# Attention weights times values: one F32 product replaced by three F32R products of rounded parts

## The chip, the cores and the metric

The kernel runs on one core of one Trainium2 chip. The metric is the device time of one execution in microseconds (us). The engines of the core are TensorE (PE, matrix products; its weight loads are listed apart as PEld), VectorE (DVE), ScalarE (ACT), GpSimd (POOL) and SyncE (SP, which issues DMAs). SBUF is the memory on the chip that the engines compute from, PSUM the one that PE writes its products to, in banks of 128 partitions x 512 F32 numbers.

## The reference, cut to what matters

One layer of an encoder over two request groups with the same weights, 2048 and 256 tokens, 2304 in all, width 1024. A projection feeds two mixers, an mLSTM with 8 heads and an attention with 8 query heads over 2 key/value heads (64 channels each), whose outputs are concatenated and projected back; then comes a feed-forward part with a convolution of width 3. The change is in the attention:

```python
def block(qi):
    s = jnp.einsum('bqhgd,bkhd->bhgqk', qi, k).astype(jnp.float32) * scale
    p = jax.nn.softmax(s, axis=-1)
    return jnp.einsum('bhgqk,bkhd->bqhgd', p.astype(v.dtype), v)
```

All of it is in float32, and attention goes over all keys of a request group.

## The kernel before, in words

The work has four phases. Phase A (`phase_a`) normalises the input and computes queries, keys, values and gates, one tile of 128 tokens after the other; it writes them to DRAM (`q_d`, `k_d`, `v_d`). Then attention (`attention`) and mLSTM (`mlstm`) run side by side as two Python generators which `run_both` advances by turns by estimated costs, the mLSTM ahead by a factor `LEAD`; once the mLSTM's program is through, steps of phase C (`phase_c`, output projection) take its place, and the attention's steps get a higher priority. Phase D (`phase_d`) is the feed-forward part. The order of instructions on each engine isn't written out: a scheduler makes it at build time from the dependencies, the priorities and a simulated timeline. On the chip each engine then takes its instructions strictly in that order, and waits on semaphores. A tile with `bufs=n` is a ring of n buffers: the next use waits for the last reader of the use n before it.

Nearly all products are made as F32R products of split operands: an operand x becomes hi = x rounded to F32R (an ACT copy into a tile of that type) and lo = x - hi (a DVE subtraction), and hi*hi + hi*lo + lo*hi are added up in PSUM. An F32 product, as the attention used for weights times values, is one call in the program, and the trace shows it as two matmul instructions with a weight load each.

The attention goes through 36 blocks of 512 queries: in each of the two key/value groups 16 large ones (one head, 4 tiles of 128 queries, 16 key tiles) and 2 small ones (two heads, 2 tiles each, 2 key tiles). `load_kv` (L440 on) brings a group's keys and values from DRAM in parts of 4 key tiles, on POOL's queue, in this order for each part: keys twice (L459), the keys' lo part (L460), values (L462). For the first large group it first writes one element of every tile (L456), which ties the loads to the end of the maxima of the first block. `vv` holds 64 channels of values and 64 columns of ones, so that a product yields the weighted sum in partitions 0 to 63 and the sum of the weights in 64 to 127.

For a block, `prep` transposes the queries, and `maxstep` (L512) makes one product of 128 queries by 512 keys (L516) and its row maximum on DVE (L517). These are done for the next block while the current one runs. `prep2` puts the negative maxima into row 64 of `qm`. `scores` (L532) takes a pair of key tiles at a time: two products each into a PSUM tile `ps` (L539, L540), then the exponential on ACT into `pe` in SBUF (L541). `values` (L544) follows `PLAG` = 2 pairs later and adds the pair to `pv` (L551). `px`, `ps`, the transposed queries and the spread maxima share a ring of `SCB` = 4 PSUM banks. At a block's end `fin1` copies sums and weight sums to SBUF (L559, L560), and `fin2`, which is called in the next block, takes the reciprocal of the weight sums on DVE (L564), multiplies on POOL (L565) and stores.

The mLSTM beside it uses one PSUM buffer (`mj`, `MJ` = 1) for its projections, which ACT copies out (L660 to L672), and short chains of small DVE, ACT and POOL steps.

Of the kernel before, what the change touches and what calls it, by code (L numbers as in the profile page):

```python
# [9 lines left out]
F32 = mybir.dt.float32  # L10
F32R = mybir.dt.float32r
AF = mybir.ActivationFunctionType
ALU = mybir.AluOpType
# [4 lines left out]
P = 128  # L18
# [4 lines left out]
NT = T // P  # L23
NT1 = T1 // P
HD = 64
# [43 lines left out]
RW = 4  # L69
PO = 4  # L70
PB = 4
PEB = 5
PLAG = 2
ZT = 3
SG = 3
# [10 lines left out]
def f32(ap):  # L86
    return ap.bitcast(F32)
# [6 lines left out]
def rstd_of(g, pool, ms, n, name):  # L94
    nc = g.nc
    r = pool.tile([P, n], F32, tag="rstd", name=name)
    nc.gpsimd.tensor_scalar(r, ms, EPS, None, ALU.add)
    nc.gpsimd.tensor_tensor(r, r, g.mhalf[:, 0:n], ALU.pow)
    return r
# [38 lines left out]
def phase_a(g, tc, sw, st_x, after_x, after_mm, after_pj):  # L138


    nc = g.nc
    with ExitStack() as st:
        sp = st.enter_context(tc.tile_pool(name="a_s", bufs=2, reuse_waits="tile"))
# [72 lines left out]
        def mm(*tiles):  # L216

            pjs = [pj_.tile([P, 1024], F32, tag="pj", name=f"pj{i}", bufs=2) for i in tiles]
            cols = ((0, 512), (512, 800))
            if tiles[0] == order[0]:  # L220
                steps = [(t, z, c) for c in range(NCC) for t in range(len(tiles)) for z in cols]
            else:
                steps = [(0, z, c) for z in cols for c in range(NCC)]
            for t, (c0, c1), c in steps:
                for k, (a, b) in enumerate(((0, 0), (0, 1), (1, 0))):
                    nc.tensor.matmul(pjs[t][:, c0:c1], nTs[tiles[t]][:, c, a, :], ws[c][:, b, c0:c1],  # L226
                                     start=(c == 0 and k == 0), stop=(c == NCC - 1 and k == 2))
            for i in tiles:
                nTs.pop(i)
            return pjs  # L230

        def post1(i, pj):
            qk = sp.tile([P, 10, HD], F32, tag="qk", name=f"qk{i}")
            nc.scalar.activation(qk, pj[:, 0:640].rearrange("p (h d) -> p h d", d=HD), AF.Copy)
            v = sp.tile([P, 2, HD], F32, tag="v", name=f"v{i}", bufs=2)
            nc.scalar.activation(v, pj[:, 640:768].rearrange("p (h d) -> p h d", d=HD), AF.Copy)
            nc.scalar.dma_start(g.v_d[:, :, i, :].rearrange("g p d -> p g d"), v)
            gt = g.gtm[:, i]
            nc.vector.tensor_tensor(gt, pj[:, 768:800].rearrange("p (a k) -> p a k", a=2),
                                    bgb.rearrange("p (a k) -> p a k", a=2), ALU.add)  # L240
            xh = sp.tile([P, 10, HD], F32, tag="xh", name=f"xh{i}", bufs=1)
            nc.scalar.activation(xh, qk, AF.Square, scale=0.125)
            ms = sp.tile([P, 10], F32, tag="ms10", name=f"ms10_{i}")
            nc.vector.tensor_reduce(ms, xh, AX.X, ALU.add)
            r = rstd_of(g, sp, ms, 10, f"rqk{i}")
            nc.vector.tensor_tensor(xh, qk, r.unsqueeze(2).to_broadcast([P, 10, HD]), ALU.mult)
            ti = i % NT1
            t1 = sp.tile([P, 10, HD], F32, tag="t1", name=f"t1_{i}")
            t2 = sp.tile([P, 10, HD], F32, tag="t2", name=f"t2_{i}", bufs=1)
            for a, (h0, h1) in enumerate(((0, 8), (8, 10))):  # L250
                n = h1 - h0
                nc.vector.tensor_tensor(t1[:, h0:h1, :], xh[:, h0:h1, :],
                                        tab[:, ti, a, 0:1, :].to_broadcast([P, n, HD]), ALU.mult)
                for q in range(2):
                    def half(t, z):
                        return t.rearrange("p h (r z f) -> p h r z f", r=2, z=2)[:, :, :, z, :]
                    sin = tab[:, ti, a, 1:2, :].rearrange("p h (r z f) -> p h r z f", r=2, z=2)[:, :, :, q, :]
                    nc.gpsimd.tensor_tensor(half(t2[:, h0:h1, :], q), half(xh[:, h0:h1, :], 1 - q),
                                            sin.to_broadcast([P, n, 2, 16]), ALU.mult)
            nc.vector.tensor_tensor(t1, t1, t2, ALU.add)  # L260
            qz = sp.tile([P, 8, P], F32R, tag="qz", name=f"qz{i}", bufs=2)
            nc.scalar.activation(qz[:, :, 0:HD], t1[:, 0:8, :], AF.Copy)
            nc.vector.tensor_tensor(qz[:, :, HD:P], t1[:, 0:8, :], f32(qz[:, :, 0:HD]), ALU.subtract)
            g.st.dma_start(g.q_d[:, i].rearrange("h p d -> p h d"), f32(qz))
            kz = sp.tile([P, 2, P], F32R, tag="kz", name=f"kz{i}", bufs=1)
            nc.scalar.activation(kz[:, :, 0:HD], t1[:, 8:10, :], AF.Copy)
            nc.vector.tensor_tensor(kz[:, :, HD:P], t1[:, 8:10, :], f32(kz[:, :, 0:HD]), ALU.subtract)
            return kz
# [41 lines left out]
        for n, i in enumerate(order):  # L310
            pj, = mm(i)
# [115 lines left out]
def attention(g, tc, s1, s2, pp):  # L427


    nc = g.nc  # L430
    sp = s1
# [8 lines left out]
    def load_kv(grp, k0, k1, after=None):  # L440

        if (grp, k0) in kv:
            return
        n = k1 - k0
        sp = s2 if n == NT1 else s1
        kv[(grp, k0)] = parts = []
        for t0 in range(0, n, 4):
            m = min(4, n - t0)
            s = f"{n}_{t0}"
            kk = sp.tile([P, m * P], F32R, tag="kk" + s, name=f"kk{grp}_{s}", bufs=1)  # L450
            kl1 = sp.tile([65, m * P], F32R, tag="kl1" + s, name=f"kl1{grp}_{s}", bufs=1)
            vv = sp.tile([P, m, P], F32, tag="vv" + s, name=f"vv{grp}_{s}", bufs=1)
            c = slice((k0 + t0) * P, (k0 + t0 + m) * P)
            if after is not None:
                for t in (kk[0:1, 0:1], kk[HD:HD + 1, 0:1], kl1[0:1, 0:1], vv[0:1, 0, 0:1]):
                    nc.gpsimd.tensor_copy(t, after[0:1, 0:1])  # L456
            nc.gpsimd.memset(vv[:, :, HD:P], 1.0)
            for r in (0, HD):
                nc.gpsimd.dma_start(f32(kk[r:r + HD, :]), g.k_d[grp, 0:HD, c])  # L459
            nc.gpsimd.dma_start(f32(kl1[0:HD, :]), g.k_d[grp, HD:P, c])  # L460
            nc.gpsimd.memset(f32(kl1[64:65, :]), 1.0)
            nc.gpsimd.dma_start(vv[:, :, 0:HD], g.v_d[grp, :, k0 + t0:k0 + t0 + m])  # L462
            parts.append((kk, kl1, vv))

    class HB:
        pass
# [64 lines left out]

    def scores(s, kp):  # L532
        N = s.N
        pe = sp.tile([P, 2, 512], F32, tag="pe", name=f"pe{s.nm}_{kp}", bufs=PEB)
        for z in range(2):
            ps = pp.tile([P, 512], F32, tag="sc", name=f"ps{s.nm}_{kp}_{z}")
            kk, kl1, _ = s.kv[kp // 2]
            kc = (2 * kp + z) % 4 * P
            nc.tensor.matmul(ps[:, 0:N], kk[:, kc:kc + P], s.qq[:, 0:N], start=True, stop=False)  # L539
            nc.tensor.matmul(ps[:, 0:N], kl1[:, kc:kc + P], s.qm[:, 0:N], start=False, stop=True)  # L540
            nc.scalar.activation(pe[:, z, 0:N], ps[:, 0:N], AF.Exp)  # L541
        return kp, pe

    def values(s, kp, pe):  # L544

        N = s.N
        if kp == 0:
            s.pv = pp.tile([P, 512], F32, tag="pv", name="pv" + s.nm, bufs=1)
        for z in range(2):
            kt = 2 * kp + z  # L550
            nc.tensor.matmul(s.pv[:, 0:N], s.kv[kp // 2][2][:, kt % 4, :], pe[:, z, 0:N], start=(kt == 0),  # L551
                             stop=(kt == s.nk - 1))

    def fin1(s):

# [5 lines left out]

    def fin2(s):
        N = s.N
        nc.vector.reciprocal(s.rs[:, 0:N], s.rs[:, 0:N])  # L564
        nc.gpsimd.tensor_tensor(s.o1[:, 0:N], s.o1[:, 0:N], s.rs[:, 0:N], ALU.mult)  # L565
        for t0, (h, q0, q1) in part(s):
            r0 = HD * (h % 2)
            nc.gpsimd.dma_start(g.mix_d[q0 // 2:q1 // 2, r0:r0 + HD, 4 + h // 2].rearrange("n p t -> p n t"),
                           s.o1[:, t0 * P:(t0 + q1 - q0) * P].rearrange("p (n t) -> p n t", t=BT))
            if h == 7:  # L570
                g.mixed.update(range(q0, q1))
# [8 lines left out]
    for n in range(len(hbs)):  # L580
# [25 lines left out]
        if nxt is not None and nxt.todo:  # L606
            while nxt.todo:
                maxstep(nxt)
            prep2(nxt)
        old, cur = cur, nxt  # L610
    fin2(old)


# [628 lines left out]
def body(tc, aps, phases="abcd"):  # L1242
    nc = tc.nc
    g = Ctx()
# [3 lines left out]
    with ExitStack() as st:  # L1248
        dp = st.enter_context(tc.tile_pool(name="dram", bufs=1, space=DRAM))
        kp = st.enter_context(tc.tile_pool(name="konst", bufs=1))  # L1250
# [4 lines left out]
        def dram(name, shape):  # L1255
            setattr(g, name, dp.tile(shape, F32, name=name))
# [4 lines left out]
        dram("x1_d", [NB, P, NCC, BT])  # L1261
        dram("q_d", [8, NT, P, P])
        dram("k_d", [2, P, T])
        dram("v_d", [2, P, NT, HD])
        dram("nm_d", [NT, 16, P])
        dram("og_d", [4, NB, P, 2, P])
        g.ident = kp.tile([P, P], F32, name="ident")
# [155 lines left out]
```

## Time and profile before

| | |
|---|---|
| Runs | 3506.89, 3509.6, 3512.7 us; median 3509.6 us |
| Profiled execution, span from first to last instruction | 3509.1 us (no other time is given for it) |
| PE busy | 3406.8 us, 97% |
| DVE busy | 2345.9 us, 67% |
| ACT busy | 1683.3 us, 48% |
| POOL busy | 1144.3 us, 33% |
| Products of weights and values (L551) | 1040 instructions, 271.9 to 1812.4 us |

How to read it: times are from one execution. A group of instructions is given as line, engine, operation, what it writes and reads, their shapes and the count; behind the first bar stand the time in which one of the group was busy and the mean duration in ns, behind the second the idle time of the engine just before them and what ended it. The ends of matmuls are modelled and overlap the next one's start, so the pace of products is read from their starts. The strips of digits are the busy share in 40 equal slices of the span, in tenths. A row of stretches has the stretch, its length, the busy time of PE, PEld, DVE, ACT and POOL (with counts of instructions), the granted PE clock as a share of full speed, the DMA engines' share and GB/s.

### The profile page before, as it was taken

Reading aid. Unit: us, or ns where it says so; the run is one execution under the profiler, and the core shown is the slowest. Engines: PE = TensorE matmul, PEld = TensorE weight load, DVE = VectorE, ACT = ScalarE, POOL = GpSimd, SP = SyncE. Lnnn points to the kernel's source line nnn. Section 1 sums busy time; section 2 is a strip of 40 time slices with the busy share of each in tenths; the row PEclk is TensorE's granted clock in tenths of the full one; section 3 lists DMA queues with packets and bytes.
Section 4 is the critical chain, followed back from the end, with each engine's and each line's share of the span. In section 5 each row is a group of like instructions: output and inputs, shape, how many; then the busy total and the mean of one; then the engine's idle time right before and its main releaser. Section 6 shows DMA issues by size and latency. Waiting matters only on the chain.

```text
span 3509.1 us, 53243 instructions
## 1 busy us (share of the span) xinstructions
PE 3406.8 (97%) x19538; PEld 3031.7 (86%) x19538; DVE 2345.9 (67%) x3962; ACT 1683.3 (48%) x3827; POOL 1144.3 (33%) x1362
## 2 busy tenths in 40 slices
PE   7889999999999999999999999999999999999998
PEld 6787787777777777767789999999999999999998
DVE  7773365546544555664444887878888879887777
ACT  5434454444444454453332544445544445655555
POOL 7863022213231322311135333224433224422222
PEclk9999999999999999999999999999999999999999
DMA  7765233233243434442247323213323213312211
GB/s 234 209 188 147 89 107 100 92 108 106 84 123 111 137 114 133 126 147 80 88 147 252 125 97 103 73 67 123 137 98 108 73 67 123 135 64 73 73 67 54
DMA packets 288917, 401.76 MB, mean 114 GB/s; under 512 B 27408, under 2 KB 188976, under 8 KB 288656
## 3 DMA queue, kind: packets, MB, share of 16 engines
q1 hardware_dynamic: 256560, 355.87, 30.9%
q0 software_dynamic: 10640, 31.86, 3.2%
q10 hardware_dynamic: 21456, 10.62, 1.0%
q8 instruction: 154, 2.52, 0.3%
q14 instruction: 107, 0.88, 0.1%
HBM read 315.55 MB, written 82.72 MB: 113 GB/s over the span
## 4 chain that ended last, share of the span: by engine, by line
PE 75%; DVE 9%; issue 5%; POOL 4%; DMA 4%; ACT 3%; SPq 0%; POOLq 0%; DVEq 0%; ACTq 0%
PE pa L1034 12%; PE pv L551 11%; PE pd L1172 11%; PE pc L1034 6%; PE po L918 5%; PE mv L668 4%; PE mj L658 4%; PE ps L539 3%; PE ps L540 3%; PE px L516 3%; PE pb L1034 3%; PE mN L794 1%; PE mj L684 1%; DVE acc L1174 1%; DVE y L1128 1%
## 5 line engine op out<-in xcount | busy, mean ns | idle before, releaser
L1172 PE MATMUL pd<-act,wd 128*128 128x384 f32 (+1 forms) x3120 | 592.0, 336 | 19.2 <-DVE acc L1174 10.8
L1172 PEld LDWEIGHTS pd<-act,wd 128*128 128x128 f32 x3120 | 540.0, 188 | 26.0 <-DVE acc L1174 14.5
L551 PE MATMUL pv<-pe,vv 128*128 128x512 f32 x1040 | 514.4, 593 | 0.2
L517 DVE TENSOR_REDUCE mx<-px 128x1 f32<-128x512 f32 (+1 forms) x528 | 342.8, 673 | 196.6 <-PE px L516 194.9
L1034 PE MATMUL pa<-nt,wut 128*128 128x386 f32 (+2 forms) x2376 | 454.7, 339 | 2.2 <-ACT u L1050 2.2
L1034 PEld LDWEIGHTS pa<-nt,wut 128*128 128x128 f32 x2376 | 422.2, 190 | 2.5 <-ACT u L1050 2.5
L541 ACT ACTIVATE pe<-ps 128x512 f32<-128x512 f32 x520 | 292.7, 595 | 266.2 <-PE ps L540 262.4
L1039 POOL TENSOR_TENSOR tw<-ru 128x512 f32<-128x512 f32 x66 | 102.1, 1547 | 740.3 <-DMA ru<-w_up 598.6
L1128 DVE SCALAR_TENSOR_TENSOR y<-u,cw,y 128x768 f32<-128x768 f32 (+1 forms) x264 | 308.9, 1171 | 35.8 <-ACT y L1121 28.8
L1174 DVE TENSOR_TENSOR acc<-pd,acc 128x384 f32<-128x384 f32 (+1 forms) x544 | 281.5, 538 | 40.1 <-PE pd L1172 38.1
L1050 ACT ACTIVATE u<-pa 128x386 f32<-128x386 f32 (+2 forms) x264 | 128.8, 488 | 328.3 <-PE pa L1034 325.8
L551 PEld LDWEIGHTS pv<-pe,vv 128*128 128x128 f32 x1040 | 189.0, 189 | 82.8 <-issue 58.3
L539 PE MATMUL ps<-qq,kk 128*128 128x512 f32 x520 | 249.5, 483 | 0.9 <-ACT pe L541 0.6
L918 PE MATMUL po<-cmx,wo 128*128 128x256 f32 x1728 | 242.5, 291 | 1.6 <-DVE wo L107 1.6
L918 PEld LDWEIGHTS po<-cmx,wo 128*128 128x128 f32 x1728 | 222.3, 191 | 24.7 <-issue 17.1
L516 PE MATMUL px<-kk,qq 128*128 128x512 f32 (+1 forms) x528 | 224.5, 455 | 2.7 <-ACT pe L541 1.3
L658 PE MATMUL mj<-mn,wm 128*128 128x256 f32 x1296 | 213.2, 305 | 8.6 <-ACT og L672 4.6
L658 PEld LDWEIGHTS mj<-mn,wm 128*128 128x128 f32 x1296 | 181.8, 194 | 38.0 <-issue 21.1
L540 PE MATMUL ps<-qm,kl 65*128 65x512 f32 x520 | 207.4, 402 | 0.1
L668 PE MATMUL mv<-wm,mn 128*128 128x256 f32 x1296 | 205.0, 298 | 0.4 <-ACT qb L664 0.4
L668 PEld LDWEIGHTS mv<-wm,mn 128*128 128x128 f32 x1296 | 178.1, 192 | 21.6 <-issue 13.9
L226 PE MATMUL pj<-w_a,n1T 128*128 128x512 f32 (+1 forms) x864 | 180.2, 363 | 8.6 <-DVE n1T L184 6.0
(285 smaller groups left out, 6663.8 us busy)
## 6 DMA issues: line engine op xcount, KB each, us to landing
ru<-w_up SPq DMA_DIRECT2D x132, 512.0 KB, 3.2
mn<-n_d SPq DMA_DIRECT2D x216, 256.0 KB, 3.3
rd<-w_down SPq DMA_DIRECT2D x66, 512.0 KB, 3.3
n_d<-n1T SPq DMA_DIRECT2D x18, 1024.0 KB, 5.2
dm<-nm_d POOLq DMA_DIRECT2D x72, 256.0 KB, 3.6
mjn<-n_d SPq DMA_DIRECT2D x72, 256.0 KB, 2.9
mvn<-n_d SPq DMA_DIRECT2D x72, 256.0 KB, 3.2
q_d<-qz SPq DMA_DIRECT2D x18, 512.0 KB, 5.6
```

The lines of the kernel that those rows point to most:

```text
L516: nc.tensor.matmul(ps[:, 0:w], s.qq[:, t * P:(t + 1) * P], s.kv[z0][0][:, 0:w], start=True, stop=True)
L517: nc.vector.tensor_reduce(s.mx[:, t, z0:z0 + 1], ps[:, 0:w], AX.X, ALU.max)
L539: nc.tensor.matmul(ps[:, 0:N], kk[:, kc:kc + P], s.qq[:, 0:N], start=True, stop=False)
L540: nc.tensor.matmul(ps[:, 0:N], kl1[:, kc:kc + P], s.qm[:, 0:N], start=False, stop=True)
L551: nc.tensor.matmul(s.pv[:, 0:N], s.kv[kp // 2][2][:, kt % 4, :], pe[:, z, 0:N], start=(kt == 0), stop=(kt == s.nk - 1))
L658: nc.tensor.matmul(pj[:, o], s.w[c][:, a, o * P:(o + 1) * P], nT[c][:, h, :], start=(c + o + k == 0), stop=(c == NCC - 1 and k == 2 and o ...
L668: nc.tensor.matmul(pv[:, o], nT[c][:, a, o * P:(o + 1) * P], s.w[c][:, h, 256:512], start=(c + o + k == 0), stop=(c == NCC - 1 and k == 2 ...
L918: nc.tensor.matmul(po[:, o], wo[c][z // 2][:, a, n], mx[c][:, h, :], start=(c == 0 and k == 0), stop=(c == NCC - 1 and k == 2))
L1034: nc.tensor.matmul(p, w[:, aa, c, :], ops[k][:, c, bb, 0:n], start=c == 0 and i == 0 and not add, stop=c == NCC // 2 - 1 and i == 2, skip_ ...
L1128: nc.vector.scalar_tensor_tensor(y[:, s:e], u[:, s + k:e + k], cw[:, k, jj:jj + 1], y[:, s:e], ALU.mult, ALU.add)
L1172: nc.tensor.matmul(po, wds[j][c // 4][:, aa, c % 4 * P:(c % 4 + 1) * P], acts[j][:, bb, z0:z1], start=(j == 0 and k == 0), stop=(j == len( ...
L1174: nc.vector.tensor_tensor(accs[c][:, z0:z1], po, accs[c][:, z0:z1], ALU.add)
```

## The change

- *Weights.* `pe` is now a ring of 3 single key tiles (it was 5 pairs, thus 10 tiles). Behind each exponential ACT copies `pe` to `x[:, 0]`, rounded to F32R, and DVE writes pe - `x[:, 0]` to `x[:, 1]`. `x` is a ring of `XB` = 6 tiles under the tag `px`.
- *Values.* Phase A rounds a tile's values on ACT and subtracts on DVE from PSUM; `v_d` holds both parts. `load_kv` loads the rounded part into `vv` and the remainder into `vl` (64 columns, no ones), with one more DMA and, where L456 applies, one more copy for each part.
- *Products.* For each key tile three F32R products are added to `pv`: `vv` by hi, `vl` by hi (into partitions 0 to 63 alone), `vv` by lo. The product of the two remainders is left out.
- *Reciprocals.* `fin2` takes the reciprocal in four pieces of 128 columns.

```diff
-PEB = 5
+PEB = 3
+XB = 6
...
-            v = sp.tile([P, 2, HD], F32, tag="v", name=f"v{i}", bufs=2)
-            nc.scalar.activation(v, pj[:, 640:768].rearrange("p (h d) -> p h d", d=HD), AF.Copy)
-            nc.scalar.dma_start(g.v_d[:, :, i, :].rearrange("g p d -> p g d"), v)
+            v = sp.tile([P, 2, 2, HD], F32R, tag="v", name=f"v{i}", bufs=2)
+            pv = pj[:, 640:768].rearrange("p (h d) -> p h d", d=HD)
+            nc.scalar.activation(v[:, :, 0], pv, AF.Copy)
+            nc.vector.tensor_tensor(v[:, :, 1], pv, f32(v[:, :, 0]), ALU.subtract)
+            nc.scalar.dma_start(g.v_d[:, :, i].rearrange("g p a d -> p g a d"), f32(v))
...
-            vv = sp.tile([P, m, P], F32, tag="vv" + s, name=f"vv{grp}_{s}", bufs=1)
+            vv = sp.tile([P, m, P], F32R, tag="vv" + s, name=f"vv{grp}_{s}", bufs=1)
+            vl = sp.tile([P, m, HD], F32R, tag="vl" + s, name=f"vl{grp}_{s}", bufs=1)
...
-            nc.gpsimd.dma_start(vv[:, :, 0:HD], g.v_d[grp, :, k0 + t0:k0 + t0 + m])
-            parts.append((kk, kl1, vv))
+            for a, t in ((0, vv[:, :, 0:HD]), (1, vl)):
+                nc.gpsimd.dma_start(f32(t), g.v_d[grp, :, k0 + t0:k0 + t0 + m, a])
+            parts.append((kk, kl1, vv, vl))
...
     def scores(s, kp):
         N = s.N
-        pe = sp.tile([P, 2, 512], F32, tag="pe", name=f"pe{s.nm}_{kp}", bufs=PEB)
+        xs = []
+        kk, kl1 = s.kv[kp // 2][0:2]
         for z in range(2):
             ps = pp.tile([P, 512], F32, tag="sc", name=f"ps{s.nm}_{kp}_{z}")
-            kk, kl1, _ = s.kv[kp // 2]
             kc = (2 * kp + z) % 4 * P
             nc.tensor.matmul(ps[:, 0:N], kk[:, kc:kc + P], s.qq[:, 0:N], start=True, stop=False)
             nc.tensor.matmul(ps[:, 0:N], kl1[:, kc:kc + P], s.qm[:, 0:N], start=False, stop=True)
-            nc.scalar.activation(pe[:, z, 0:N], ps[:, 0:N], AF.Exp)
-        return kp, pe
+            pe = sp.tile([P, 512], F32, tag="pe", name=f"pe{s.nm}_{kp}_{z}", bufs=PEB)
+            x = sp.tile([P, 2, 512], F32R, tag="px", name=f"xx{s.nm}_{kp}_{z}", bufs=XB)
+            nc.scalar.activation(pe[:, 0:N], ps[:, 0:N], AF.Exp)
+            nc.scalar.activation(x[:, 0, 0:N], pe[:, 0:N], AF.Copy)
+            nc.vector.tensor_tensor(x[:, 1, 0:N], pe[:, 0:N], f32(x[:, 0, 0:N]), ALU.subtract)
+            xs.append(x)
+        return kp, xs
...
-            nc.tensor.matmul(s.pv[:, 0:N], s.kv[kp // 2][2][:, kt % 4, :], pe[:, z, 0:N], start=(kt == 0),
-                             stop=(kt == s.nk - 1))
+            nc.tensor.matmul(s.pv[:, 0:N], vv[:, kt % 4, :], x[:, 0, 0:N], start=kt == 0, stop=False)
+            nc.tensor.matmul(s.pv[0:HD, 0:N], vl[:, kt % 4, :], x[:, 0, 0:N], start=False, stop=False)
+            nc.tensor.matmul(s.pv[:, 0:N], vv[:, kt % 4, :], x[:, 1, 0:N], start=False, stop=kt == s.nk - 1)
...
-        nc.vector.reciprocal(s.rs[:, 0:N], s.rs[:, 0:N])
+        for t in range(s.nq):
+            c = slice(t * P, (t + 1) * P)
+            nc.vector.reciprocal(s.rs[:, c], s.rs[:, c])
...
-        dram("v_d", [2, P, NT, HD])
+        dram("v_d", [2, P, NT, 2, HD])
```

More of the change, by code (lines that the diff above doesn't have):

```diff
@@ L451, in load_kv @@
             kl1 = sp.tile([65, m * P], F32R, tag="kl1" + s, name=f"kl1{grp}_{s}", bufs=1)
-            vv = sp.tile([P, m, P], F32, tag="vv" + s, name=f"vv{grp}_{s}", bufs=1)
+            vv = sp.tile([P, m, P], F32R, tag="vv" + s, name=f"vv{grp}_{s}", bufs=1)
+            vl = sp.tile([P, m, HD], F32R, tag="vl" + s, name=f"vl{grp}_{s}", bufs=1)
             c = slice((k0 + t0) * P, (k0 + t0 + m) * P)
             if after is not None:
-                for t in (kk[0:1, 0:1], kk[HD:HD + 1, 0:1], kl1[0:1, 0:1], vv[0:1, 0, 0:1]):
+                for t in (kk[0:1, 0:1], kk[HD:HD + 1, 0:1], kl1[0:1, 0:1], vv[0:1, 0, 0:1], vl[0:1, 0, 0:1]):
                     nc.gpsimd.tensor_copy(t, after[0:1, 0:1])
-            nc.gpsimd.memset(vv[:, :, HD:P], 1.0)
+            nc.gpsimd.memset(f32(vv[:, :, HD:P]), 1.0)
             for r in (0, HD):
@@ L540, in scores, with values @@
             nc.tensor.matmul(ps[:, 0:N], kl1[:, kc:kc + P], s.qm[:, 0:N], start=False, stop=True)
-            nc.scalar.activation(pe[:, z, 0:N], ps[:, 0:N], AF.Exp)
-        return kp, pe
-    def values(s, kp, pe):
+            pe = sp.tile([P, 512], F32, tag="pe", name=f"pe{s.nm}_{kp}_{z}", bufs=PEB)
[5 more added lines that the diff above has]
+        return kp, xs
+    def values(s, kp, xs):
         N = s.N
@@ L548, in values @@
             s.pv = pp.tile([P, 512], F32, tag="pv", name="pv" + s.nm, bufs=1)
-        for z in range(2):
+        vv, vl = s.kv[kp // 2][2:4]
+        for z, x in enumerate(xs):
             kt = 2 * kp + z
-            nc.tensor.matmul(s.pv[:, 0:N], s.kv[kp // 2][2][:, kt % 4, :], pe[:, z, 0:N], start=(kt == 0),
-                             stop=(kt == s.nk - 1))
+            nc.tensor.matmul(s.pv[:, 0:N], vv[:, kt % 4, :], x[:, 0, 0:N], start=kt == 0, stop=False)
+            nc.tensor.matmul(s.pv[0:HD, 0:N], vl[:, kt % 4, :], x[:, 0, 0:N], start=False, stop=False)
+            nc.tensor.matmul(s.pv[:, 0:N], vv[:, kt % 4, :], x[:, 1, 0:N], start=False, stop=kt == s.nk - 1)
     def fin1(s):
```

## The prediction

> **What bounds the kernel now.** I read the page's busy shares and slices first, then its chain of waits, then busy time by stretches, then groups with shapes kept apart, and single instructions last.
>
> ```profile
> span 3509.1 us, 53243 instructions
> ...
> PE 3406.8 (97%) x19538; PEld 3031.7 (86%) x19538; DVE 2345.9 (67%) x3962; ACT 1683.3 (48%) x3827; POOL 1144.3 (33%) x1362
> ...
> PE   7889999999999999999999999999999999999998
> ...
> DVE  7773365546544555664444887878888879887777
> ACT  5434454444444454453332544445544445655555
> ...
> PEclk9999999999999999999999999999999999999999
> ...
> PE 75%; DVE 9%; issue 5%; POOL 4%; DMA 4%; ACT 3%; SPq 0%; POOLq 0%; DVEq 0%; ACTq 0%
> PE pa L1034 12%; PE pv L551 11%; PE pd L1172 11%; PE pc L1034 6%; PE po L918 5%; PE mv L668 4%; PE mj L658 4%; PE ps L539 3%; PE ps L540 3%; PE px L516 3%; PE pb L1034 3%; PE mN L794 1%; PE mj L684 1%; DVE acc L1174 1%; DVE y L1128 1%
> ```
>
> TensorE is the bound, at an undiminished clock, and the products that the change replaces (`pv`, L551) hold 11% of the chain. A modelled busy share could hide gaps, so the stretches come next; columns are PE, weight loads, DVE, ACT, POOL busy, then clock and DMA.
>
> ```profile
> 0.00:300.00 300.00, 255.62 (x1464) 221.58 (x1464) 215.11 (x364) 133.82 (x233) 215.63 (x309) 0.95 0.72 211
> 300.00:1100.00 800.00, 796.54 (x4472) 625.05 (x4473) 383.93 (x825) 371.19 (x1051) 183.32 (x367) 1.00 0.32 99
> 1100.00:1600.00 500.00, 490.51 (x2677) 376.39 (x2676) 298.17 (x712) 244.71 (x703) 126.10 (x248) 1.00 0.41 129
> ...
> 300.00:1800.00 1500.00, 1487.05 (x8273) 1157.23 (x8274) 773.38 (x1690) 690.99 (x1896) 337.99 (x643) 1.00 0.34 107
> 1500.00:1600.00 100.00, 94.61 (x489) 70.69 (x488) 63.22 (x139) 49.55 (x123) 15.93 (x26) 0.98 0.38 123
> 1900.00:2000.00 100.00, 88.47 (x500) 86.28 (x500) 87.44 (x111) 54.09 (x96) 49.18 (x30) 0.97 0.52 180
> 2000.00:2400.00 400.00, 396.94 (x2249) 394.99 (x2248) 317.22 (x439) 186.89 (x343) 124.66 (x84) 1.00 0.25 87
> ```
>
> ```profile
> L551 PE MATMUL pv<-pe,vv x1040: 590/592/697, 271.9 to 1812.4; 128*128 128x512 f32 x174
> ```
>
> By this row (least, median and longest duration, then first and last start) attention runs from 272 to 1813 us. In its 1500 us from 300 on, PE is idle 1500 - 1487.05 = 13 us, DVE is busy 52%, ACT 46%. So a shorter PE stream shortens the kernel there one for one, for as long as DVE and ACT keep up. The last three rows are my gauges for what a busier DVE does to PE: at 63% DVE PE lost 5.4% in one stretch, at 79% only 0.8% over 400 us, at 87% 11.5%.
>
> **The products.** 2 key/value groups x (16 large blocks x 16 key tiles + 2 small x 2) = 520 key tiles of 128 keys x 512 queries. One F32 product is two instructions in the trace.
>
> ```profile
> L551 PE MATMUL pv<-pe,vv 128*128 128x512 f32 x1040 | 514.4, 593 | 0.2
> L551 PEld LDWEIGHTS pv<-pe,vv 128*128 128x128 f32 x1040 | 189.0, 189 | 82.8 <-issue 58.3 <-ACT rs L560 1.1 <-ACT qq L504 0.7
> ```
> ```profile
> 701.49 0.40 PE L539 MATMUL ps<-qq,kk 128*128 128x512 f32 x1
> 701.73 0.40 PE L540 MATMUL ps<-qm,kl 65*128 65x512 f32 x1
> 701.97 0.39 PE L539 MATMUL ps<-qq,kk 128*128 128x512 f32 x1
> 702.20 0.39 PE L540 MATMUL ps<-qm,kl 65*128 65x512 f32 x1
> ```
> ```profile
> 1101.61 1.88 PE L551 MATMUL pv<-pe,vv 128*128 128x512 f32 x4
> 1103.33 0.38 PE L718 MATMUL mt<-ident,mkT 128*128 128x128 f32 x2
> ```
>
> Durations overlap, so I price by starts. Four F32 instructions take 1103.33 - 1101.61 = 1.72 us, 0.43 each, 0.86 a key tile. F32R products of the same 512 columns (the scores) start every (702.20 - 701.49)/3 = 0.237 us. Three of them take 0.71. Removed 1040 x 0.43 = 447 us, added 1560 x 0.237 = 370: **-77 us**. The weight loads, 189 ns each, stay shorter than a product. No F32R product here writes half the partitions (`vl` has 64 columns); the 65-row one costs the same 0.237, so I price it full. The gain would be gone at 447/1560 = 0.287 per product.
>
> **What ACT and DVE get.**
>
> ```profile
> L517 DVE TENSOR_REDUCE mx<-px 128x1 f32<-128x512 f32 x512 | 336.8, 682 | 187.1 <-PE px L516 185.4
> L541 ACT ACTIVATE pe<-ps 128x512 f32<-128x512 f32 x520 | 292.7, 595 | 266.2 <-PE ps L540 262.4
> ...
> L658 PE MATMUL mj<-mn,wm 128*128 128x256 f32 x1296 | 213.2, 305 | 8.6 <-ACT og L672 4.6 <-DMA mn<-n_d 3.9
> ...
> L1031 DVE TENSOR_TENSOR wut<-ru,wut 128x512 fp32r<-128x512 f32 x132 | 103.0, 780 | 42.3 <-ACT wut L1030 41.9 <-issue 0.3
> ...
> L1224 DVE TENSOR_TENSOR wd<-rd,wd 128x512 fp32r<-128x512 f32 x128 | 94.6, 760 | 0.0
> ...
> L1223 ACT ACTIVATE wd<-rd 128x512 fp32r<-128x512 f32 x128 | 74.3, 619 | 9.9 <-PE pd L1172 9.9
> L1031 DVE TENSOR_TENSOR wu<-tw,wu 128x512 fp32r<-128x512 f32 x66 | 64.1, 972 | 6.8 <-ACT wu L1030 6.6
> ```
>
> The rounded copy is the form of L1223, 0.62 us: 520 x 0.62 = 322 us on ACT, 691 + 322 = 1013 of 1500 - 77 = 1423 us, 71%. The remainder is the form of L1224, 0.76 us; the same subtraction costs from 0.78 to 0.97 at L1031. 520 x 0.76 = 395 us on DVE. I take the low end because POOL is busy only 338/1500 = 23% in this stage. DVE then stands at 773 + 395 + 16 (reciprocals, below) = 1184 of 1423, 83%; at 0.97 it would be 1293, 91%. All of it is hidden behind PE while PE is the bound; uncovered, it would cost more than the change gives.
>
> The new wait: an exponential needs one of three `pe` halves, and the one of three key tiles earlier comes free only when DVE has subtracted from it; before, DVE stood nowhere in that loop and there were ten halves. Behind a waiting exponential on ACT stand its copies out of PSUM for the mLSTM projections; L658 waits for such a copy (one `mj` buffer), so PE would stop. On DVE the subtraction queues behind maxima of 0.68 us and the mLSTM's chains. The other side has slack: a product is due two key-tile pairs after its scores, 1500/260 = 5.8 us a pair, while exponential, copy and subtraction of a pair take 2 x (0.60 + 0.62) = 2.4 us on ACT and 1.5 on DVE; the six `px` tiles are three pairs, so a copy waits only for products of three pairs earlier, which stand ahead of these scores on PE.
>
> How much idle this adds to PE no row shows. Lower bound: the 0.8% of 2000-2400 (DVE 79%), 11 us against today's 13, **-2**. Upper: the 5.4% of 1500-1600 throughout, 77 us, **+64**. I take 2.5%, 35 us, **+22**: PE loses nothing in 300-1100 except 3.5 us, but 9.5 of 500 us in 1100-1600, where the mLSTM's short dependent steps share DVE, and that second part should suffer most.
>
> **Reciprocals.**
>
> ```profile
> L564 DVE RECIPROCAL rs<-rs 64x512 f32<-64x512 f32 x36 | 120.2, 3340 | 87.8 <-ACT rs L560 87.6
> ...
> L799 DVE RECIPROCAL dn<-dn 128x4 f32<-128x4 f32 x72 | 12.6, 175 | 1.7
> ```
>
> (3340 - 175)/508 = 6.2 ns a column; a piece of 128 is 175 + 124 x 6.2 = 0.95 us, four are 3.8, so 36 x 0.45 = 16 us more on DVE, hidden in its idle 17%. They bring shorter blocking: 0.95 instead of 3.3 us, if something is put between the pieces. On PE's 13 us of idle that can give a few us at most; with 83% on DVE it is what keeps the subtraction from coming late. I count 0.
>
> **Values and their loads.**
>
> ```profile
> L820 DVE TENSOR_TENSOR mmx<-mT,ogT x18: 251/282/292, 1431.5 to 1550.6; 128x128 f32<-128x128 f32 x18
> ```
> ```profile
> L462 POOL DMA_DIRECT2D vv<-v_d x10: 724/775/828, 256.1 to 1037.7; - x10
> L456 POOL COPY vv<-m x4: 173/173/174, 263.2 to 270.7; 1x1 f32<-1x1 f32 x4
> ```
>
> In the first 300 us, 18 subtractions from PSUM of 0.28 us (L820's form) put 5 us on DVE, ahead of the gate addition and the head-norm chain of the same tile, whose end PE's transposes wait for. DVE is 72% busy there: 0 to +5, taken +2. The store from ACT's queue doubles in bytes and issues as often. On POOL's queue ten more loads of 0.78 us and four copies of 0.17 push the keys of the second, third and fourth part of a group back by 1, 2 and 3 us, in two places (about 265 and 1035 us); PE has projections to do there: 0 to +6, taken +2.
>
> **Sum**, against the profiled execution's 3509.1 us (0.5 below the runs' median 3509.6, which I neglect): 3509.1 - 77 + 22 + 2 + 2 = **3458**. Its own range is 3509.1 - 77 - 2 = 3430 to 3509.1 - 77 + 64 + 11 = 3507.
>
> **Rivals.**
>
> 1. *The stalls eat the gain.* PE loses throughout what it lost in 1500-1600: 3509.1 - 77 + 64 + 4 = 3500. For it: that stretch had DVE at 63% only. Against: 2000-2400 ran at 79% with 0.8%.
>
> 2. *DVE late, ACT stopped, slower than before.* The ring of three `pe` halves ties ACT to DVE. If subtractions cost 0.97, DVE stands at 91%, and PE idles as in 1900-2000 (DVE 87%, PE 11.5% idle): 0.115 x 1423 = 164 us, 151 more than now: 3509.1 - 77 + 151 + 4 = 3587. It decides from 77 us added, 0.15 us for each key tile. For it: L1031 at 972 ns. Against: that form's source is made by POOL just before, and 1900-2000 also has a change of phase with the DMA at 0.52.
> The Trainium skill, GPSIMD Engine Reference, Key points, speaks for this rival: GpSimd shares its SBUF interfaces with VectorE and contends with DVE instructions that have two SBUF inputs, which every new subtraction is and the maxima, read from PSUM, are not. By that rule the trace agrees where POOL's product feeds the subtraction (972 against 760 ns); applied to all 520 it is the 91% above.
>
> 3. *It doesn't do what it says*: the accumulating triple starts no faster than 0.287 us a product, or the F32 pair hid work that now shows. Then 3509.1 + 4 = 3513. Against: the scores, equal in type and width, hold 0.237 with a new weight load each.
>
> **Chances.** Forecast 0.72, rival 1 0.11, rival 2 0.12, rival 3 0.05. A measurement of this kernel can tell about 0.2%, 7 us, from no change. Below 3502.6: nearly all of the forecast and half of rival 1, 0.75. Within: 0.08. Above 3516.6: rival 2 and the overrun of rivals 1 and 3, 0.17. Range 3420 (all of today's 13 us of idle gone too) to 3540, which holds the forecast, rivals 1 and 3 and the mild end of rival 2.
>
> **What would show it.** Right: L551's three products start 0.23 to 0.24 us apart; attention ends near 1760 instead of 1813; the later phases keep their length; DVE is near 83% and ACT near 71% in the stage, PE's idle between 1 and 5%. Wrong: the chain of waits or PE's idle in the stage names the subtraction, or exponentials idle before DVE; subtractions average above 0.9 us; or the triple is slower than 0.25.

## The result and the profile after

The changed kernel takes 3461.1 us (median of four runs, 3455.2 to 3464.5) where the kernel before takes 3510.3 (3506.9 to 3512.7): a ratio of 0.9863, with a 95% interval of 0.9848 to 0.9877, or 49 us. The forecast was 3458 in 3420 to 3540. The profiled execution is the shortest of the four: the runs are compared by medians, the traces by spans.

The page after, cut to the lines that answer to those of before:

```profile
span 3453.4 us, 55887 instructions
...
PE 3331.2 (96%) x20058; PEld 3093.4 (90%) x20058; DVE 2680.4 (78%) x4608; ACT 1952.9 (57%) x4347; POOL 1183.8 (34%) x1376
...
PE   7989999999999999999998999999999999999998
...
DVE  7875687778767787887756888888888878878776
ACT  4535666666666677565644444446544446555555
...
PE 71%; DVE 12%; issue 5%; POOL 5%; ACT 4%; DMA 4%; SPq 0%; POOLq 0%; ACTq 0%; DVEq 0%
```

PE is still the bound, with 4 points less of the chain than before, 3 of which DVE has taken. DVE's strip in slices 4 to 20, attention, rose from mostly 4 to 6 tenths to 6 to 8, ACT's from 4 and 5 to mostly 6. The stretches of the kernel after (stretch, length, then PE, PEld, DVE, ACT and POOL busy):

```profile
0.00:300.00 300.00, 253.97 (x1503) 221.35 (x1504) 227.74 (x393) 137.12 (x239) 228.22 (x318) 0.97 0.73 219
300.00:1100.00 800.00, 787.88 (x4930) 685.70 (x4928) 583.61 (x1217) 536.04 (x1376) 206.05 (x380) 1.00 0.35 107
1100.00:1600.00 500.00, 482.11 (x2913) 408.06 (x2913) 400.06 (x898) 329.74 (x859) 140.28 (x249) 0.99 0.41 127
300.00:1740.00 1440.00, 1409.98 (x8742) 1218.13 (x8741) 1085.16 (x2287) 949.53 (x2397) 368.22 (x648) 1.00 0.36 113
```

From 300 to 1740 us PE is idle 30 us, 2.1%, where it was idle 13 us in 1500; DVE is at 75%, ACT at 66%. Where the gain lies is told by first and last starts. First the values' products and the first product of phase D after, then phase D's before:

```profile
L562 PE MATMUL pv<-xx,vv x520: 387/391/586, 274.1 to 1763.8; 128*128 128x512 f32 x174
...
L1048 PE MATMUL pa<-n,wu x792: 331/338/668, 1851.9 to 3389.1; 128*128 128x386 f32 x66, 128*128 128x384 f32 x66, 128*128 128x382 f32 x66
```
```profile
L1034 PE MATMUL pa<-n,wu x792: 331/338/668, 1906.8 to 3444.9; 128*128 128x386 f32 x66, 128*128 128x384 f32 x66, 128*128 128x382 f32 x66
```

Attention starts 2 us later (274 for 272), phase D 55 us earlier, and phase D is as long as it was: 3453.4 - 1851.9 = 1601.5 for 1602.3. So 54.9 of the 55.7 us between the spans come from what stands before phase D, and there from the stretch with attention, which got 57 us shorter while phase A got 2 longer. Single instructions there show the new pace; a product of `vl` is one of three:

```profile
340.92 0.40 PE L564 MATMUL pv<-xx,vv 128*128 128x512 f32 x1
341.15 0.39 PE L562 MATMUL pv<-xx,vv 128*128 128x512 f32 x1
341.38 0.39 PE L563 MATMUL pv<-xx,vl 128*64 128x512 f32 x1
341.61 0.39 PE L564 MATMUL pv<-xx,vv 128*128 128x512 f32 x1
341.83 0.40 PE L562 MATMUL pv<-xx,vv 128*128 128x512 f32 x1
342.07 0.39 PE L563 MATMUL pv<-xx,vl 128*64 128x512 f32 x1
342.30 0.38 PE L732 MATMUL mt<-ident,mkT 128*128 128x128 f32 x2
```

Six products in 342.30 - 340.92 = 1.38 us, 0.230 each. And the groups that are new or paid for it:

```profile
L550 DVE TENSOR_TENSOR xx<-pe,xx 128x512 fp32r<-128x512 f32 x520 | 370.8, 725 | 165.6 <-ACT xx L549 161.3 <-PE mu L751 0.8 <-PE mv L682 0.6
L549 ACT ACTIVATE xx<-pe 128x512 fp32r<-128x512 f32 x520 | 316.2, 633 | 4.7
L548 ACT ACTIVATE pe<-ps 128x512 f32<-128x512 f32 x520 | 298.6, 595 | 151.1 <-PE ps L545 136.2 <-DVE mx L522 4.0 <-DVE xx L550 2.1
L564 PE MATMUL pv<-xx,vv 128*128 128x512 f32 x520 | 214.1, 412 | 12.4 <-DVE xx L550 12.2
...
L578 DVE RECIPROCAL rs<-rs 64x128 f32<-64x128 f32 x144 | 122.5, 902 | 8.9 <-ACT rs L572 7.9 <-POOL rcol_c L133 0.5 <-issue 0.4
```

The wait that is new on PE stands in L564, the product with the remainder: 12.2 us until the subtraction is through.

**Idle by starts.** A matmul's modelled end covers part of each gap that follows it, so I also priced every PE instruction between the first product of values and the first of phase D by the usual distance of starts of its form (0.428 us for an F32 instruction of 512 columns, 0.232 and 0.119 for F32R of 512 and 256, and so on), and called idle what lies between the priced end of one and the start of the next, if above 30 ns. This is the balance, in us, for all traces of this study; the stretch goes from the first product of values to the first product of phase D, so a few us of other work can fall in or out. `after_again` is the changed kernel run once more, beside the second group of experiments, as a yardstick for them; the other labels are those of the sections below:

```
kernel            stretch   work   idle   runs' median, ratio to before (95% interval)
before             1634.9 1595.9   33.2   3510 to 3512
after              1577.9 1509.3   64.7   3461.1  0.9863 (0.9848 to 0.9877)
after_again        1579.6 1509.3   67.0   3462.9  0.9865 (0.9849 to 0.9882)
parts_unread       1663.6 1595.9   61.7   3541.3  1.0081 (1.0064 to 1.0099)
products_only      1564.8 1512.7   48.4   3442.6  0.9797 (0.9784 to 0.9811)
before_recip4      1634.5 1595.9   33.3   3511.2  0.9996 (0.9987 to 1.0006)
recip_whole        1584.3 1509.3   71.4   3463.6  0.9870 (0.9856 to 0.9885)
sub_half_twice     1634.4 1509.3  121.6   3516.4  1.0005 (0.9994 to 1.0015)
copy_half_twice    1613.4 1509.3  100.2   3487.2  0.9926 (0.9911 to 0.9941)
two_products       1508.2 1388.6  115.1   3392.6  0.9652 (0.9637 to 0.9668)
lo_late            1587.7 1509.3   74.9   3470.3  0.9889 (0.9874 to 0.9904)
sub_pool           1576.5 1509.3   63.5   3463.4  0.9869 (0.9847 to 0.9892)
ring2              1584.3 1509.3   71.2   3464.8  0.9868 (0.9853 to 0.9883)
exp_twice          1589.0 1506.9   77.9   3472.9  0.9891 (0.9875 to 0.9908)
```

So the change took 87 us of work off PE and gave 31 of them back as idle. Most of that idle has one place: priced in this way, 22 of the 31 us stand in front of the values' products, about 16 of them before L564, whose weight load waits for the subtraction (us in all, times, longest):

```profile
PEld pv L564 <- DVE xx L550: 23.6, 30, 3.0
```

### The profile page after: what moved, and what is told of

Its sections match the earlier page's. It is cut to its first block, busy times and chain, and to the rows that moved or that the text cites. A ratio compares the mean times of both kernels' runs of the same rounds, so it can differ in the third digit from the quotient of the medians.

```text
span 3453.4 us, 55887 instructions
## 1 busy us (share of the span) xinstructions
PE 3331.2 (96%) x20058; PEld 3093.4 (90%) x20058; DVE 2680.4 (78%) x4608; ACT 1952.9 (57%) x4347; POOL 1183.8 (34%) x1376
## 4 chain that ended last, share of the span: by engine, by line
PE 71%; DVE 12%; issue 5%; POOL 5%; ACT 4%; DMA 4%; SPq 0%; POOLq 0%; ACTq 0%; DVEq 0%
PE pa L1048 13%; PE pd L1186 12%; PE pc L1048 7%; PE po L932 5%; PE mj L672 4%; PE mv L682 4%; PE ps L544 3%; PE pb L1048 3%; PE ps L545 3%; PE pv L564 3%; PE pv L562 3%; PE pv L563 3%; PE px L521 3%; DVE mx L522 1%; PE mN L808 1%
## 5 line engine op out<-in xcount | busy, mean ns | idle before, releaser
L550 DVE TENSOR_TENSOR xx<-pe,xx 128x512 fp32r<-128x512 f32 x520 | 370.8, 725 | 165.6 <-ACT xx L549 161.3
L548 ACT ACTIVATE pe<-ps 128x512 f32<-128x512 f32 x520 | 298.6, 595 | 151.1 <-PE ps L545 136.2
L549 ACT ACTIVATE xx<-pe 128x512 fp32r<-128x512 f32 x520 | 316.2, 633 | 4.7
L932 PEld LDWEIGHTS po<-cmx,wo 128*128 128x128 f32 x1728 | 230.7, 190 | 18.1 <-ACT wo L106 1.0
L564 PE MATMUL pv<-xx,vv 128*128 128x512 f32 x520 | 214.1, 412 | 12.4 <-DVE xx L550 12.2
L544 PE MATMUL ps<-qq,kk 128*128 128x512 f32 x520 | 212.9, 412 | 1.3 <-ACT pe L548 0.9
L562 PE MATMUL pv<-xx,vv 128*128 128x512 f32 x520 | 209.1, 402 | 1.9 <-ACT xx L549 1.3
L563 PE MATMUL pv<-xx,vl 128*64 128x512 f32 x520 | 206.5, 397 | 0.0
L672 PE MATMUL mj<-mn,wm 128*128 128x256 f32 x1296 | 198.8, 286 | 7.3 <-ACT og L686 4.8
```

Of the source, the lines that this page charges most:

```text
L549: nc.scalar.activation(x[:, 0, 0:N], pe[:, 0:N], AF.Copy)
L550: nc.vector.tensor_tensor(x[:, 1, 0:N], pe[:, 0:N], f32(x[:, 0, 0:N]), ALU.subtract)
L562: nc.tensor.matmul(s.pv[:, 0:N], vv[:, kt % 4, :], x[:, 0, 0:N], start=kt == 0, stop=False)
L564: nc.tensor.matmul(s.pv[:, 0:N], vv[:, kt % 4, :], x[:, 1, 0:N], start=False, stop=kt == s.nk - 1)
L672: nc.tensor.matmul(pj[:, o], s.w[c][:, a, o * P:(o + 1) * P], nT[c][:, h, :], start=(c + o + k == 0), stop=(c == NCC - 1 and k == 2 and o ...
L932: nc.tensor.matmul(po[:, o], wo[c][z // 2][:, a, n], mx[c][:, h, :], start=(c == 0 and k == 0), stop=(c == NCC - 1 and k == 2))
```

## The experiments

### Parts made, old product

The kernel before, which makes the parts and reads none of them:

```diff
             nc.scalar.activation(pe[:, z, 0:N], ps[:, 0:N], AF.Exp)
+            x = sp.tile([P, 2, 512], F32R, tag="px", name=f"xx{s.nm}_{kp}_{z}", bufs=XB)
+            nc.scalar.activation(x[:, 0, 0:N], pe[:, z, 0:N], AF.Copy)
+            nc.vector.tensor_tensor(x[:, 1, 0:N], pe[:, z, 0:N], f32(x[:, 0, 0:N]), ALU.subtract)
```

> The kernel before, with the F32 product kept, and the rounded copy (ACT) and the remainder (DVE) of every exponential made as in the change but read by nobody. Theory: PE's stream is the bound and unchanged, the 520 copies and 520 subtractions hide behind it but cost PE the 17 us of idle that the changed kernel's attention shows over the kernel before: 3525 to 3532 us. Rival, the parts are free and the idle has another cause: 3510 us. Rival, the parts cost far more than 20 us and the products save far more than 80: 3550 us or more.

Measured 3541.3 us, a ratio of 1.0081, some 28 us above before: between the theory's 3525 to 3532 and the rival's 3550, and plainly not free. PE's work is that of before to the tenth of a us; its idle grew from 33 to 62. No product on PE reads the parts here, and the stretch still got 29 us longer, so the added work costs by making other things late. The largest growth, 13 of the 28 us of idle by starts, stands before `px` and `ps`, 8.2 us before and 21 here: they wait for banks of the PSUM ring that ACT and DVE empty. The rest is spread over the small products of the mLSTM and the queries. Work on engines that were half idle wasn't hidden.

### Products alone

```diff
-            pe = sp.tile([P, 512], F32, tag="pe", name=f"pe{s.nm}_{kp}_{z}", bufs=PEB)
...
-            nc.scalar.activation(pe[:, 0:N], ps[:, 0:N], AF.Exp)
-            nc.scalar.activation(x[:, 0, 0:N], pe[:, 0:N], AF.Copy)
-            nc.vector.tensor_tensor(x[:, 1, 0:N], pe[:, 0:N], f32(x[:, 0, 0:N]), ALU.subtract)
+            nc.scalar.activation(x[:, 0, 0:N], ps[:, 0:N], AF.Exp)
...
-            nc.tensor.matmul(s.pv[:, 0:N], vv[:, kt % 4, :], x[:, 1, 0:N], start=False, stop=kt == s.nk - 1)
+            nc.tensor.matmul(s.pv[:, 0:N], vv[:, kt % 4, :], x[:, 0, 0:N], start=False, stop=kt == s.nk - 1)
```

> The changed kernel without the parts: the exponential writes the rounded tile itself, there is no copy and no subtraction, and the third product multiplies the rounded tile once more, so the remainder of the weights is left out of the sum. Theory: the three products alone are worth 447 - 370 = 77 us or, at the 0.231 us now seen, 80 us, and nothing adds idle: 3510 - 80 + 4 = about 3434 us. Rival, the parts cost nothing and the products save only the 49 us measured: 3461 us. Rival, parts dear and products worth more: below 3415 us.

Measured 3442.6 us, 71 us below before by its ratio (0.9797), 9 short of the 3434 expected. The work fell by 83 us as priced, but idle rose by 15 although nothing was added to DVE or ACT. The stretch of this kernel and that of the kernel with the parts unread:

```profile
300.00:1700.00 1400.00, 1374.53 (x8542) 1195.75 (x8541) 756.82 (x1756) 675.62 (x1868) 336.83 (x642) 1.00 0.38 113
```
```profile
300.00:1800.00 1500.00, 1477.06 (x8110) 1140.09 (x8108) 1073.63 (x2178) 943.56 (x2384) 358.87 (x636) 0.99 0.36 106
```

With DVE at 757/1400 = 54% PE loses 25 of 1400 us, with DVE at 72% it loses 23 of 1500. So here a shorter PE stream over the same chains on the other engines idles more by itself. The two halves together, -71 and +28, make -43; the change measured -49.

### Reciprocals, one way and the other

The kernel before with the loop of `fin2` from the change, and the changed kernel without it:

```diff
-        for t in range(s.nq):
-            c = slice(t * P, (t + 1) * P)
-            nc.vector.reciprocal(s.rs[:, c], s.rs[:, c])
+        nc.vector.reciprocal(s.rs[:, 0:N], s.rs[:, 0:N])
```

> The kernel before with only the reciprocal in four pieces. Theory: DVE is half idle in the stage and PE has 13 us of idle there, so it is worth between 0 and -5 us: 3505 to 3511 us. Rival, the 3.3 us reciprocal holds up much on DVE and the pieces are a main part of the gain: 3490 us or less.

> The changed kernel with the reciprocal in one piece again. Theory, as forecast: worth nothing to a few us, since products come two pairs late and one reciprocal of 3.3 us in a block of 41 us rarely reaches PE: 3461 to 3467 us. Rival, the pieces are what lets DVE carry the subtractions: 3475 us or more.

Both as the theory had it, within the noise: 0.9996 (0.9987 to 1.0006) against before, and 3463.6 us where the changed kernel ran 3462.9 on the same chip. The pieces are worth nothing that can be measured in either kernel.

### More on DVE, more on ACT

Every second subtraction twice, and in another kernel every second copy twice:

```diff
-            nc.vector.tensor_tensor(x[:, 1, 0:N], pe[:, 0:N], f32(x[:, 0, 0:N]), ALU.subtract)
+            for _ in range(1 + z):
+                nc.vector.tensor_tensor(x[:, 1, 0:N], pe[:, 0:N], f32(x[:, 0, 0:N]), ALU.subtract)
```
```diff
-            nc.scalar.activation(x[:, 0, 0:N], pe[:, 0:N], AF.Copy)
+            for _ in range(1 + z):
+                nc.scalar.activation(x[:, 0, 0:N], pe[:, 0:N], AF.Copy)
```

> The changed kernel with every second subtraction done twice, 260 x 0.73 = 190 us more on DVE and nothing else. Theory: DVE goes from 75% to 88% of the stage, near the 87% at which PE lost 11.5% in a stretch of the kernel before, so PE idles 5 to 10% of 1440 us instead of 2%: 3500 to 3575 us. Rival, DVE's cover is wide because products come two pairs late: 3461 to 3475 us.

> The changed kernel with every second rounded copy done twice, 260 x 0.63 = 164 us more on ACT and nothing else; the counterpart of the doubled subtractions, which cost 55 us for 190 us on DVE. Theory A, PE's idle comes from DVE, at 75%, rather than from ACT, at 65%: 3463 to 3480 us. Theory B, any busy engine in the loop costs PE the same, 0.29 us for each us added: about 3510 us.

The doubled subtractions cost 55 us, all of the gain and more: 3516.4 against 3461.1. Their group, and the product that waits, in that kernel:

```profile
L551 DVE TENSOR_TENSOR xx<-pe,xx 128x512 fp32r<-128x512 f32 x780 | 545.9, 715 | 115.3 <-ACT xx L549 109.5 <-PE ps L545 1.6
...
L565 PE MATMUL pv<-xx,vv 128*128 128x512 f32 x520 | 217.6, 418 | 22.7 <-DVE xx L551 22.2
```

545.9 - 370.8 = 175 us more on DVE, 55 us lost by the medians, 49 by the ratios to before (1.0005 - 0.9865): 0.28 to 0.31 us for each. DVE stood at 82% of the stretch from 300 to 1800 us (1236 of 1500), less than the 88% expected, since the stretch grew too. The doubled copies put 474.2 - 316.2 = 158 us on ACT and cost 3487.2 - 3461.1 = 26 us by the medians, 21 by the ratios (0.9926 - 0.9865): 0.14 to 0.17 for each. That lies between theory A (up to 3480) and B (3510): work on either engine costs PE time, on DVE about twice as much for a us. Both doublings also make each second remainder come later, and no run separates that delay from the load on the engine.

### One product less

```diff
-            nc.tensor.matmul(s.pv[0:HD, 0:N], vl[:, kt % 4, :], x[:, 0, 0:N], start=False, stop=False)
```

> The changed kernel without the product of the values' remainder, which is left out of the sum: 520 products of 0.231 us less, 120 us. Theory: PE's pace is the bound, but a shorter PE stream over the same DVE and ACT work idles more, as the run with the products alone showed with 15 us more for 83 us less: 3463 - 120 + 15 to 35 = 3358 to 3378 us. Rival, DVE and ACT bound the stage by now: 3400 us or more.

Measured 3392.6 us: 70 of the 120 us came, and neither theory's range holds it. Work fell by 1509.3 - 1388.6 = 121 us, so the price of a product holds; idle went from 65 to 115. The rival's bound isn't reached either: the stage does get shorter, at 58 us for 100. PE alone is no longer the bound of this stage in the sense that its time comes off one for one.

### Four tries at the idle

The product with the remainder moved behind the next step of the other generators (`lows`, a new function that makes this product, called in front of the next `scores` and at the block's end):

```diff
-            nc.tensor.matmul(s.pv[:, 0:N], vv[:, kt % 4, :], x[:, 1, 0:N], start=False, stop=kt == s.nk - 1)
+        s.late = (kp, xs)
...
         for kp in range(nkp):
+            lows(cur)
             todo.append(scores(cur, kp))
```

> The changed kernel with the remainder's product of a key tile pair moved behind the next step of the other generators (in front of the next scores), same buffers. Theory: of the 65 us that PE loses in attention and what follows up to phase D, worked out from its starts, 23 us are waits of products for a remainder; a later place takes most of them away: 3440 to 3452 us. Rival, the idle only moves, since DVE's queue and not the place is what is late: 3457 to 3465 us.

Every fourth subtraction on POOL:

```diff
-            nc.vector.tensor_tensor(x[:, 1, 0:N], pe[:, 0:N], f32(x[:, 0, 0:N]), ALU.subtract)
+            (nc.gpsimd if (2 * kp + z) % 4 == 3 else nc.vector).tensor_tensor(
+                x[:, 1, 0:N], pe[:, 0:N], f32(x[:, 0, 0:N]), ALU.subtract)
```

> The changed kernel with every fourth subtraction on POOL instead of DVE: 130 x 0.72 = 94 us off DVE, 130 x about 1.5 us = 195 us onto POOL, which is 26% busy. Theory: less on DVE means fewer late remainders, if POOL's own are on time: 3445 to 3460 us. Rival, POOL and DVE contend for SBUF and POOL's masks for the mLSTM come late: 3465 to 3500 us.

A ring of two `pe` halves (`PEB = 2`):

> The changed kernel with two pe halves instead of three, so that an exponential waits for the subtraction of two key tiles before. Theory: the ring is no bound (in the changed kernel's trace exponentials idle 2 us before subtractions): 3460 to 3468 us. Rival, the tie of ACT to DVE through the ring is behind the added idle: 3475 us or more.

The rounded part from a second exponential:

```diff
-            nc.scalar.activation(x[:, 0, 0:N], pe[:, 0:N], AF.Copy)
+            nc.scalar.activation(x[:, 0, 0:N], ps[:, 0:N], AF.Exp)
```

> The changed kernel with the rounded part made by a second exponential from PSUM instead of a copy from SBUF: 520 x (0.632 - 0.595) = 19 us less on ACT, and the two ACT steps no longer depend on each other, but the PSUM bank is held 0.6 us longer. Theory: worth nothing, since the products come two pairs late: 3455 to 3470 us. Rival, banks are the limit: 3475 us or more; rival, the dependent steps on ACT cost PE time: 3445 us or less.

None of them is faster than the changed kernel. `lo_late` took 3470.3 us, 7 more than the changed kernel beside it, with intervals that just overlap: the theory fell, and even the rival's range (to 3465) is missed. This is the wait in the kernel with the later products, then in the changed kernel (us in all, times, longest):

```profile
PE pv L575 <- DVE xx L550: 6.4, 8, 1.6
```
```profile
PE pv L564 <- DVE xx L550: 12.2, 12, 2.5
```

The named wait is halved and the idle as a whole grew from 65 to 75 us: it moved. By starts, what stands before the values' products fell by 2 us only, and what stands before `ps` rose by 7.

`sub_pool` measured 3463.4, the same as the changed kernel beside it, and between the ranges of theory and rival. The move freed little: its 128 recorded subtractions on POOL take 1.37 us each, those left on DVE 0.782 instead of 0.725 (0.684 with no POOL instruction beside them, 0.98 for the 114 that POOL overlaps for more than half), and other DVE instructions beside POOL got longer too. DVE's busy time from 300 to 1740 us fell from 1085 to 1064 us, 21 where 94 were expected:

```profile
L550 DVE TENSOR_TENSOR xx<-pe,xx 128x512 fp32r<-128x512 f32 x392 | 303.0, 782 | 176.6 <-ACT xx L549 172.9 <-PE mj L673 1.9 <-PE pv L564 0.5
...
300.00:1740.00 1440.00, 1410.73 (x8733) 1221.94 (x8732) 1064.13 (x2172) 960.86 (x2411) 538.70 (x779) 0.99 0.37 111
```

So this run doesn't tell what less work on DVE would be worth.

`ring2` is within noise of the changed kernel (0.9868), so the tie of ACT to DVE through the ring isn't what costs. `exp_twice` is slower by some 9 us (0.9891 for 0.9865), again with intervals that just overlap, and with less on ACT (911 us from 300 to 1740 for 950): in that kernel PE waits for the second exponential to free a bank.

```profile
PE px L521 <- ACT xx L549: 7.1, 9, 2.7
```

That points to the rival that names the banks, just short of its price (3475 or more expected, 3472.9 measured).

## Why the prediction was right

The time, 3461 for 3458, was right, and by steps mostly for the reason given. Two terms were off by about 10 us each, in opposite directions; that they cancel is luck.

**The bound.** PE set the pace of the stage, and what left its stream shortened the kernel: shown by the products alone (-71 us), while the parts without the products made it slower (+28).

**The products** (-77): mis-sized. Priced by the rows' 0.43 and 0.237 they were to save 77; by the new trace's pace of 0.230 to 0.232 it is 447 - 1560 x 0.231 = 87, and the balance shows 87 after and 83 with the products alone. That `vl` costs a full product though it fills half the partitions was right (0.23 in the rows above).

**The added idle** (+22, between -2 and +64): mis-sized, 31 by starts. By the busy rows, the measure that I took the gauges from, it was 35 expected and 30 measured; that measure hides part of every gap. The reason behind the number was half right. Late remainders do hold up PE: in the changed kernel's trace about half of the added idle stands before L564. But the products alone idle 15 us more without any remainder, and the parts alone cost 28 without a reader. The way in which DVE was to make PE idle, by its ring of `pe` and the exponentials stopped behind it, is not what the trace shows (below). The gauges, idle shares of other stretches by their DVE load, were a poor instrument: the stage as a whole loses 2.1% with DVE at 75%, less than half of what 1500 to 1600 us lost with DVE at 63%. So DVE's load alone doesn't set the loss. The same work runs about 50 us earlier in the changed kernel and loses 7.7% there, with DVE at 83% and the granted clock at 0.95 for 0.98:

```profile
1452.00:1552.00 100.00, 92.31 (x504) 74.86 (x503) 82.66 (x179) 65.12 (x151) 17.85 (x24) 0.95 0.35 111
```

**Loads of DVE and ACT.** A copy was 0.63 us for 0.62, a subtraction 0.725 for 0.76. DVE came to 75%, not 83, that is 1085 us for 1184. Half of the 99 us lie at the subtractions, which add about 343 us of busy time in the stage for 395 counted: 9 of the 520 fall outside it, each is shorter, and an instruction's end overlaps the next one's start. Reciprocals take 122.5 us in all for 120.2 before, so 2 us more instead of 16 (a piece is 0.90 for 0.95, and they overlap too). The rest is spread over the other groups. ACT came to 66% for 71 in the same way.

The 0.97 us of L1031, on which rival 2 rests, is a mean of two kinds: in the trace before, 41 of the 66 run with no POOL instruction beside them and take 0.69 us, 24 are overlapped by POOL for more than half and take 1.47. A POOL instruction at the same time goes with the long ones, not a source that POOL made: `wu<-ru`, whose sources come from DRAM, shows the same two kinds, 99 of 0.69 us alone and 25 of 1.26 under POOL.

**The ring of three halves**, on which rival 2 was built: wrong as a danger. L548 idles 2.1 us in the whole run before a subtraction, and a ring of two changed nothing. **Reciprocals** (0) were right, in both directions. **Values and loads** (+4): of the right size on average. Attention starts 2 us later in this trace, 274.1 for 271.9; over all traces it starts at 269.7 to 271.9 us in the three kernels with the old values (mean 270.9) and at 269.9 to 279.6 in the eleven with the new (mean 275.1).

**Rivals.** That the stalls eat the gain and that the kernel gets slower did not come, but `sub_half_twice` shows how near they were: some 175 us more on DVE, as with subtractions of 1.06 us instead of 0.725, would have left nothing. The forecast of slower at 0.97 us a subtraction would have needed 151 us of idle; at the measured 0.3 for each us, 520 x (0.97 - 0.725) = 127 us would cost about 40, an estimate that no run tests. Rival 3, a triple that starts no faster, is refuted by the rows at 341 us.

**Open:** which mechanism turns load on DVE and ACT into idle on PE. The wait for the remainder carries about half of it in the changed kernel, yet halving that wait in `lo_late` gained nothing. The order on each engine is fixed at build time by a simulated timeline, and instructions that come later on the chip than there would produce just such scattered waits, but no run here tests that. Two nearby rivals weren't run either: products that follow more than two pairs behind their scores (`PLAG`), which would tell lateness from load, and a longer ring of `x` (`XB`).

## What to carry to other kernels

An F32 product of 512 columns costs 0.86 us in two instructions, three F32R ones 0.69: in this kernel, where ACT and DVE had room for the rounded parts, the split form was faster by 49 us. "Hidden" work on half-idle engines isn't free: in this stage, with DVE at 75% and ACT at 65%, each us added cost about 0.3 and 0.15 us. The price is steep at the margin: the parts themselves, 371 us on DVE and 316 on ACT, cost 19 us (3461.1 - 3442.6), and 175 more on DVE cost 49 to 55. Each us taken from PE alone came back only in part (0.86 of it at first, 0.58 at the next step), so a gain on the bound has to be priced with the idle that it makes. A wait's own size is no measure of what its removal gives.

## What the runs showed of the hardware

A subtraction of two SBUF operands depends on POOL. This is its form in the changed kernel (least, median, longest), and POOL's multiplication of `o` by the reciprocals, first before and then after:

```profile
L550 DVE TENSOR_TENSOR xx<-pe,xx x520: 617/685/1792, 271.3 to 1762.5; 128x512 fp32r<-128x512 f32 x174
```
```profile
L565 POOL TENSOR_TENSOR o<-o,rs 64x512 f32<-64x512 f32 x36 | 46.5, 1292 | 159.8 <-DVE rs L564 150.8 <-DVE m4r L525 5.8 <-DVE m L523 3.0
```
```profile
L579 POOL TENSOR_TENSOR o<-o,rs 64x512 f32<-64x512 f32 x36 | 54.2, 1506 | 151.4 <-ACT xx L549 77.8 <-DVE rs L578 52.6 <-issue 9.2
```

About 350 subtractions with no POOL instruction beside them take 0.685 us on average, the 130 that POOL overlaps for more than half 0.83, the longest 1.79; POOL's multiplication went from 1.29 to 1.51 us. By the contention of GpSimd with two-operand SBUF instructions of VectorE (the Trainium skill, GPSIMD Engine Reference, Key points) the trace agrees in both directions; with POOL 26% busy it cost 21 us of DVE in all (520 x 0.040, the mean of 0.725 less 0.685), far from the 91% load that rival 2 made of it. With a fourth of the subtractions on POOL, what DVE instructions took longer beside POOL ate most of what the move freed (`sub_pool`).

A weight load of 64 columns takes 0.134 us for the 0.188 of 128 (least to longest 133 to 139 and 186 to 193), while the product behind it costs the same. And before the weight loads of the F32 products stood 58 us of idle that no instruction explains, in 241 pieces of 0.24 us. The other two kernels with F32 products have 37 and 55 us there (`parts_unread`, `before_recip4`), those with F32R products in their place none. The F32 products themselves didn't wait for it: PE idles 0.2 us before all of L551.
